# A fixed order of VectorE's work at the ends of sub-layers, and ten early products of constants, in a two-layer trunk

## The chip, the cores and the metric

The kernel runs on one core of one Trainium2 chip. Its time is the device time of one launch, in microseconds. Three runs of the kernel before took 2077.28, 2075.53 and 2076.88 us; the median is 2076.88 us. One more execution was recorded by the hardware profiler; it took 2074.67 us, and the trace spans 2072.9 us of that. Engines are called PE (matrix products; PEld is its weight load), DVE (VectorE), ACT (ScalarE), POOL (GpSimd) and SP (which here only issues transfers).

## The reference

A trunk of two layers works on x of 256 rows and 2048 columns in float32. Each layer has a mixer and a squared-ReLU MLP, and each of these four sub-layers ends in the same way:

```python
h = rms_norm(x, mix_pre_g[layer])
m = pool_conformer_mixer(...) if layer % 2 == 0 else short_conv_mixer(...)
x = x + rms_norm(m, mix_post_g[layer])
h = rms_norm(x, ffn_pre_g[layer])
x = x + rms_norm(sq_relu_mlp(h, ffn_w1[layer], ffn_w2[layer]), ffn_post_g[layer])
```

The first mixer projects h into three parts: one goes through causal means over 2, 4, 8 and 16 frames and a small product, the other two through a gate, a causal depthwise convolution of width 31, LayerNorm and swish; both results go through one output projection. The second mixer is `W_out(B * conv3(C * u))`. The MLP is 2048 to 8192 to 2048 with `relu(.)**2` between. `rms_norm` needs the sum of squares over a whole row of 2048, so no column of the next sub-layer can be started before the last column of this one is known.

## The kernel before, in words

The 256 rows are two tiles of 128 (`t` is 0 or 1, called row 0 and row 1 here). Every large product takes float32 operands as two parts, a high part `hi` and the remainder `lo`, and adds up three products: high by high, high by low and low by high (lines 224 to 226). Weights are streamed in segments of 128 x 1024 floats (512 KB): `prep_to` (L166) issues the transfer into `raw` on SP's queue (L170), ACT copies it to `whi` (L173), DVE subtracts to make `wlo` (L178; in part of the first mixer POOL does it). There are four `raw` buffers and nine of `whi` and `wlo` each. A block of 512 output columns of one row tile is one call of `mms`: three matmuls of 512 columns for each of its 8 or 16 pieces of 128 input rows, so 24 or 48 matmuls.

The order on each engine is not written by hand. The program is traced in Python order, and a scheduler then lays the instructions out by a model of their times: on each engine it takes the ready instruction of highest priority, which is the earliest traced one; `urgent` (L329) raises what it wraps by 150 places. The resulting queues are static and every engine works in order. `later` and `tick` (L197, L201) put small tasks, such as transposes, between the matmuls of following blocks.

At the end of a sub-layer, for each row tile, `mix_evac` or `last_evac` (L587, L654) handles each block of 512 columns: a sum of squares on ACT, and a product by the gain on DVE into `m` (L592 or L659). After the last block `mix_close` (L594) makes the row's factor: a square root on ACT and six small DVE operations (L600, L320 to L324). `close_row` (L343) then updates x in four pieces of 512 columns on DVE (L355), and for each piece `norm_chunk` (L293) has PE transpose it in four matmuls (L276), ACT write the high part `xh` (L262) and DVE the remainder `xl` (L265). The last blocks of a sub-layer are ordered so that row 0 is done 10.9 us of matmuls before row 1. The next sub-layer's first block is row 0's, by `mms_wide` (L229), which takes all products with the weights' high parts first (L240, L241), and those with the low parts last (L248). There are three such ends inside the run (layer 0's mixer, layer 0's MLP, layer 1's mixer), called ends A, B and C here, and the end of the program.

In layer 0's mixer, `pool_sum` (L448) forms the causal means by products with a constant matrix, multiplies by `inv_cnt` on DVE (L463) into an SBUF tile, splits that (`split_plain`, L270: ACT L271, DVE L272), and `pool_mix` (L478) multiplies the two parts (L492). `ln_stats` and `ln_apply` do the LayerNorm with products by a constant matrix `ones` of 1/1024 (L547, L560). The last projection of this mixer adds a block to its earlier part in `opart` (L647) and goes over the column blocks and row tiles in the order (2,0), (2,1), (3,0), (3,1), (0,0), (1,0), (0,1), (1,1).

Of the kernel before, what the change touches and what calls it, by code (L numbers as in the profile page):

```python
# [16 lines left out]
P = 128  # L17
# [16 lines left out]
def trunk_kernel(  # L34
# [19 lines left out]

    uid = [0]
# [103 lines left out]
    pool_lo = set()  # L159
    for key in ("f1_0_0_0", "sC0", "f1_1_0_0"):  # L160
        pool_lo |= set()
# [4 lines left out]
    def prep_to(i):  # L166
        while nxt[0] <= min(i, len(specs) - 1):
            src, nj = specs[nxt[0]]
            raw = wp.tile([P, 2 * CB], F32, tag="raw", name=nm("raw"), bufs=4)
            nc.sync.dma_start(raw.rearrange("p (j n) -> p j n", j=nj), src)  # L170
            hi = wp.tile([P, 2 * CB], F32R, tag="whi", name=nm("whi"))
            lo = wp.tile([P, 2 * CB], F32R, tag="wlo", name=nm("wlo"))
            act.copy(hi, raw)  # L173
            i_, on_pool = nxt[0], nxt[0] in pool_lo

            def low(raw=raw, hi=hi, lo=lo, on_pool=on_pool, eng=lo_eng[0](i_)):
                for s in ((slice(0, CB), slice(CB, 2 * CB)) if on_pool else (slice(None),)):
                    (pool if on_pool else eng).tensor_tensor(  # L178
                        lo[:, s], raw[:, s], hi.bitcast(F32)[:, s], ALU.subtract)

            low()
            wt[i_] = (hi, lo)
            nxt[0] += 1

    AHEAD = 8
    URGENT = 150
# [70 lines left out]
    def split_cols(p, col0, dst, scale_cols):  # L257

        hi, lo = dst
        for j in range(4):  # L260
            pj = p[:, j * P : (j + 1) * P]
            act.activation(hi[:, col0 + j, :], pj, AF.Copy, scale=scale_cols[j])  # L262
        for j in range(4):
            pj = p[:, j * P : (j + 1) * P]
            dve.scalar_tensor_tensor(  # L265
                lo[:, col0 + j, :], pj, scale_cols[j], hi[:, col0 + j, :].bitcast(F32),
                ALU.mult, ALU.subtract,
            )

# [23 lines left out]
    def norm_chunk(t, c, gkey, gbase):  # L293
        p = pst()
        transpose4(xs[t][:, c * CB : (c + 1) * CB], p)
        split_cols(p, 4 * (c % 2), xT[t, c // 2], [pcol(gkey, gbase + 4 * c + j) for j in range(4)])
# [46 lines left out]
    def close_row(t, s, nxt_gain, final=False):  # L343
# [3 lines left out]
        for c in range(4):  # L347
            cs = slice(c * CB, (c + 1) * CB)
            if final and c == 0:
                for q in (slice(0, CB // 2), slice(CB // 2, CB)):  # L350
                    dve.scalar_tensor_tensor(xs[t][:, q], ms[t][:, q], s, xs[t][:, q],
                                             ALU.mult, ALU.add)
                    nc.sync.dma_start(out[t * P : (t + 1) * P, q], xs[t][:, q])
                continue
            dve.scalar_tensor_tensor(xs[t][:, cs], ms[t][:, cs], s, xs[t][:, cs], ALU.mult, ALU.add)  # L355
# [23 lines left out]

    first()  # L380
# [59 lines left out]
    def load_pool():  # L440
        for s in range(2):
            raw = wp.tile([P, 2 * CB], F32, tag="raw", name=nm("rw"), bufs=4)
# [3 lines left out]
            pwin.append(w)  # L446

    def pool_sum(g):  # L448

        ic = t512((P, T))  # L450
        nc.sync.dma_start(ic, inv_cnt[g * T : (g + 1) * T].partition_broadcast(P))
        p = pst()
        for c in range(2):
# [8 lines left out]
        pd = t512((P, 2, T))  # L462
        dve.tensor_tensor(  # L463
            pd, p.rearrange("p (c n) -> p c n", c=2),
            ic.unsqueeze(1).to_broadcast([P, 2, T]), ALU.mult,
        )
        ph = tp.tile([P, 2, T], F32R, tag="ph", name=nm("ph"), bufs=2)
        pl = tp.tile([P, 2, T], F32R, tag="pl", name=nm("pl"), bufs=2)
# [125 lines left out]
    def mix_close(t, parts, nxt_gain, final=False):  # L594
# [7 lines left out]
        close_row(t, r, nxt_gain, final)  # L602
# [32 lines left out]
    for cb, t in ((2, 0), (2, 1), (3, 0), (3, 1), (0, 0), (1, 0), (0, 1), (1, 1)):  # L635
# [7 lines left out]
        else:  # L643
# [3 lines left out]
            dve.tensor_tensor(o, ps, o, ALU.add)  # L647
            ps = o
        urgent(mix_evac, t, cb, ps, gps[cb], parts)
        if cb == 1:  # L650
            urgent(mix_close, t, parts, ("ffn_pre", 0))
# [9 lines left out]
    def ffn(l, nxt_gain, final=False):  # L661
# [5 lines left out]
        for e in range(NE):  # L667
# [33 lines left out]
            for cb, t in order:  # L701
# [14 lines left out]
                if cb == NCB - 1:  # L716
                    urgent(mix_close, t, parts, nxt_gain, final)
# [63 lines left out]
    for cb in range(NCB):  # L781
        ids = seg[f"so{cb}"]
        gp = post_gain(mix_post_g, 1, cb)
        for t in range(NT):
# [4 lines left out]
            if cb == NCB - 1:  # L789
                urgent(mix_close, t, parts, ("ffn_pre", KT))  # L790
# [44 lines left out]
```

## Time and profile before

| what | value |
|---|---|
| median of 3 runs | 2076.88 us (2075.53 to 2077.28) |
| profiled execution: time, span of the trace | 2074.67 us, 2072.9 us |
| mean granted PE clock | 0.995 |
| PE busy, PEld busy | 2041.4 us (98%), 1687.7 us (81%) |
| DVE, ACT, POOL busy | 1174.0 us (57%), 1008.3 us (49%), 153.5 us (7%) |
| transfers | 390.30 MB at 188 GB/s mean |
| matmuls recorded | 9253 |

The trace's times are microseconds from its first instruction. A duration of a matmul in the trace is longer than the distance to the next one, since matmuls are pipelined; the price of a matmul is therefore read from the distance between starts. In the rows of waits, the engine and line that waited stand left of the arrow and what it waited for stands right of it.

### The profile page before, as it was taken

What the parts mean: (1) busy time and instruction counts of PE and PEld (TensorE: products, weight loads), DVE (VectorE), ACT (ScalarE), POOL (GpSimd) and SP (SyncE); (2) the same over time, 40 slices, a digit from 0 to 9 for tenths busy, and PEclk for the clock granted to TensorE, in tenths of its full rate; (3) what the DMA queues carried; (4) which work ended last, traced back from release to release, by engine and by line L of the source; (5) the groups of instructions that cost most, each with busy time, mean ns of one, the idle gap of its engine ahead of it and who ended that gap; (6) DMA issues with size and microseconds to landing.
All of it is one profiled execution on the core that took longest, in us unless ns stands there. A gap on an engine that the chain in (4) does not pass through costs nothing.

```text
span 2072.9 us, 24556 instructions
## 1 busy us (share of the span) xinstructions
PE 2041.4 (98%) x9253; PEld 1687.7 (81%) x9253; DVE 1174.0 (57%) x1522; ACT 1008.3 (49%) x1296; POOL 153.5 (7%) x83
## 2 busy tenths in 40 slices
PE   8999999999999999999999999999999999999998
PEld 7888778888888888887888888888888888888886
DVE  3797764455455455547655645674555464554545
ACT  6454664444444354445544444464544444353443
POOL 5887000000000000000000000000000000000000
PEclk9999999999999999999999999999999999999999
DMA  7665546556565556556454665655555565565653
GB/s 261 198 208 180 176 148 219 175 180 210 171 203 181 184 194 198 186 170 213 161 197 165 201 197 177 202 189 193 183 193 193 170 212 187 171 208 189 201 172 114
DMA packets 203078, 390.30 MB, mean 188 GB/s; under 512 B 12368, under 2 KB 14512, under 8 KB 202960
## 3 DMA queue, kind: packets, MB, share of 16 engines
q1 hardware_dynamic: 202656, 388.55, 56.7%
q8 instruction: 72, 1.18, 0.2%
q14 instruction: 46, 0.38, 0.1%
q0 software_dynamic: 256, 0.18, 0.0%
q10 hardware_dynamic: 48, 0.02, 0.0%
HBM read 386.60 MB, written 2.10 MB: 188 GB/s over the span
## 4 chain that ended last, share of the span: by engine, by line
PE 85%; DVE 2%; DMA 1%; issue 1%; ACT 0%; DVEq 0%; ACTq 0%
PE pg L224 27%; PE pg L226 27%; PE pg L225 27%; PE pt L276 2%; DVE wlo L178 1%; DVE x L355 1%; PE pg L248 1%; PE pg L241 0%; DMA gp<-in_mix_post_g_dram 0%; PE pg L240 0%; DMA raw<-in_ab_w_out_dram 0%; ACT whi L173 0%; DVE xl L265 0%; DMA raw<-in_sc_w_in_dram 0%; DVE m L592 0%
## 5 line engine op out<-in xcount | busy, mean ns | idle before, releaser
L178 DVE TENSOR_TENSOR wlo<-raw,whi 128x1024 fp32r<-128x1024 f32 x660 | 807.5, 1227 | 580.4 <-ACT whi L173 547.9
L173 ACT CAST whi<-raw 128x1024 fp32r<-128x1024 f32 x722 | 760.2, 1054 | 575.2 <-PE pg L226 383.1
L226 PE MATMUL pg<-whi,xl 128*128 128x512 f32 x1520 | 596.0, 393 | 0.0
L224 PE MATMUL pg<-whi,xh 128*128 128x512 f32 x1520 | 590.9, 390 | 0.8 <-ACT t L518 0.7
L225 PE MATMUL pg<-wlo,xh 128*128 128x512 f32 x1520 | 591.3, 390 | 0.0
L225 PE MATMUL pg<-wlo,ah 128*128 128x512 f32 x1024 | 398.3, 389 | 0.0
L224 PE MATMUL pg<-whi,ah 128*128 128x512 f32 x1024 | 398.1, 389 | 0.0
L226 PE MATMUL pg<-whi,al 128*128 128x512 f32 x1024 | 397.6, 391 | 0.0
L225 PEld LDWEIGHTS pg<-wlo,xh 128*128 128x128 f32 x1520 | 285.4, 188 | 59.1
L224 PEld LDWEIGHTS pg<-whi,xh 128*128 128x128 f32 x1520 | 285.5, 188 | 58.5 <-ACT t L518 1.1
L226 PEld LDWEIGHTS pg<-whi,xl 128*128 128x128 f32 x1520 | 285.4, 188 | 56.9
L225 PEld LDWEIGHTS pg<-wlo,ah 128*128 128x128 f32 x1024 | 192.2, 188 | 40.1
L224 PEld LDWEIGHTS pg<-whi,ah 128*128 128x128 f32 x1024 | 192.3, 188 | 39.3
L226 PEld LDWEIGHTS pg<-whi,al 128*128 128x128 f32 x1024 | 192.3, 188 | 39.3
L178 POOL TENSOR_TENSOR wlo<-raw,whi 128x1024 fp32r<-128x1024 f32 x62 | 147.7, 2421 | 46.4 <-ACT whi L173 46.1
L680 ACT ACTIVATE t<-pg,rr 128x512 f32<-128x512 f32 x64 | 43.9, 686 | 194.0 <-PE pg L226 192.8
L711 DVE TENSOR_TENSOR m<-pg,m 128x512 f32<-128x512 f32 x96 | 65.9, 687 | 74.6 <-PE pg L226 74.6
L224 PE MATMUL pg<-whi,yh 128*128 128x512 f32 x256 | 100.2, 392 | 1.6 <-ACT yh L271 1.5
L225 PE MATMUL pg<-wlo,yh 128*128 128x512 f32 x256 | 99.7, 390 | 0.0
L226 PE MATMUL pg<-whi,yl 128*128 128x512 f32 x256 | 98.5, 390 | 0.2 <-DVE yl L272 0.2
L421 DVE SCALAR_TENSOR_TENSOR acc<-pp,par,acc 128x256 f32<-128x256 f32 x240 | 96.3, 480 | 0.1
L272 DVE TENSOR_TENSOR al<-pt,ah 128x512 fp32r<-128x512 f32 x64 | 44.0, 688 | 74.8 <-ACT ah L271 74.7
(130 smaller groups left out, 902.9 us busy)
## 6 DMA issues: line engine op xcount, KB each, us to landing
raw<-in_ffn_w_dram SPq DMA_DIRECT2D x512, 512.0 KB, 4.7
raw<-in_sc_w_in_dram SPq DMA_DIRECT2D x96, 512.0 KB, 4.9
raw<-in_ab_w_in_dram SPq DMA_DIRECT2D x48, 512.0 KB, 4.6
raw<-in_ab_w_out_dram SPq DMA_DIRECT2D x32, 512.0 KB, 3.9
raw<-in_sc_w_out_dram SPq DMA_DIRECT2D x32, 512.0 KB, 5.4
x<-in_x_dram SPq DMA_DIRECT2D x8, 256.0 KB, 7.2
gp<-in_mix_post_g_dram SPq DMA_DIRECT2D x8, 256.0 KB, 5.9
gp<-in_ffn_post_g_dram SPq DMA_DIRECT2D x8, 256.0 KB, 4.6
```

What stands on the lines that cost most here:

```text
L173: act.copy(hi, raw)
L178: (pool if on_pool else eng).tensor_tensor(lo[:, s], raw[:, s], hi.bitcast(F32)[:, s], ALU.subtract)
L224: pe.matmul(ps, lh, wh, start=start and k == 0, stop=False)
L225: pe.matmul(ps, lh, wl, start=False, stop=False)
L226: pe.matmul(ps, ll, wh, start=False, stop=stop and k == n - 1)
L248: pe.matmul(ps, lhs(k)[0], wt[c][1][:, j * CB : (j + 1) * CB], start=False, stop=k == n - 1)
L272: dve.tensor_tensor(lo, src, hi.bitcast(F32), ALU.subtract)
L276: pe.transpose(p[:, j * P : (j + 1) * P], src[:, j * P : (j + 1) * P], ident)
L355: dve.scalar_tensor_tensor(xs[t][:, cs], ms[t][:, cs], s, xs[t][:, cs], ALU.mult, ALU.add)
L421: dve.scalar_tensor_tensor(a, src, wcol, a, ALU.mult, ALU.add)
L680: act.activation(rl, ps, AF.Relu, scale=rr[t])
L711: dve.tensor_tensor(dst, ps, dst, ALU.add)
```

## The change

- At the three inner ends, DVE gets a fixed order by scheduling edges that cost no semaphore. Of the nine weight segments that come first in the next sub-layer, `wlo` of numbers 1 to 4 come after row 0's second x update, and those of numbers 5 to 8 after the last remainder `xl` of row 0; row 1's first x update also comes after that last remainder. Number 0 is left free.
- `urgent` raises by 1000 places and not by 150, and now also wraps L647, which writes its sum into the PSUM bank and not into `opart`.
- There are six `raw` buffers. The first two segments of the next sub-layer at ends A and B take their `hi` and `lo` from the three buffers of tags `ah` and `al`, which hold activations elsewhere.
- `inv_cnt` is loaded in `load_pool`, two transfers in place of four, into the two buffers that the post gains use; `pool_sum` multiplies inside the PSUM bank, and its parts `ph` and `pl` lie among the `t512` tiles.
- The last projection of layer 0's mixer goes (2,0), (3,0), (2,1), (3,1), and then as before.
- Before the first transfers have landed, PE gets ten products of `ones` by `ones` into a bank that nothing reads.
- After the row factors of the start, a one-column sigmoid on ACT.

```diff
-            raw = wp.tile([P, 2 * CB], F32, tag="raw", name=nm("raw"), bufs=4)
+            raw = wp.tile([P, 2 * CB], F32, tag="raw", name=nm("raw"), bufs=RAW)      # RAW = 6
...
-            hi = wp.tile([P, 2 * CB], F32R, tag="whi", name=nm("whi"))
-            lo = wp.tile([P, 2 * CB], F32R, tag="wlo", name=nm("wlo"))
+            home, tags = (ap_, ("ah", "al")) if nxt[0] in guests else (wp, ("whi", "wlo"))
+            hi = home.tile([P, 2 * CB], F32R, tag=tags[0], name=nm("whi"))
+            lo = home.tile([P, 2 * CB], F32R, tag=tags[1], name=nm("wlo"))
...
+    guests = set(seg["f1_0_0_0"][:2]) | set(seg["sC0"][:2])
+    def after(inst, first):
+        tc.add_manual_dep(
+            inst.ins, first.ins.name,
+            mybir.DependencyInfo(mybir.DependencyClass.NoSync, mybir.DependencyReason.SCHED_ONLY),
+            reason="row chain first")
+    def hold(ids, first):
+        for i in ids:
+            if i in lows:
+                after(lows[i], first)
+            else:
+                guards[i] = first
...
-    URGENT = 150
+    URGENT = 1000
...
-            dve.scalar_tensor_tensor(xs[t][:, cs], ms[t][:, cs], s, xs[t][:, cs], ALU.mult, ALU.add)
+            upd = dve.scalar_tensor_tensor(xs[t][:, cs], ms[t][:, cs], s, xs[t][:, cs],
+                                           ALU.mult, ALU.add)
+            if nxt_ids:
+                if t == 0 and c == 1:
+                    hold(nxt_ids[1:5], upd)
+                if t == NT - 1 and c == 0:
+                    after(upd, split_end[0])
...
+                    end = urgent(norm_chunk, t, c, *nxt_gain)
+                    if t == 0 and c == 3:
+                        split_end[0] = end
+                        hold(nxt_ids[5:], end)
...
+    idle = pst()
+    for i in range(10):
+        pe.matmul(idle[:, :P], ones, ones, start=i == 0, stop=i == 9)
     first()
...
     for t in range(NT):
         row_scale(t)
+    act.activation(small(), rr[NT - 1], AF.Sigmoid)
...
+        for h in range(2):
+            ic = mp.tile([P, 2 * T], F32, tag="gp", name=nm("ic"))
+            nc.sync.dma_start(ic, inv_cnt[2 * h * T : 2 * (h + 1) * T].partition_broadcast(P))
...
-        pd = t512((P, 2, T))
-        dve.tensor_tensor(
-            pd, p.rearrange("p (c n) -> p c n", c=2),
-            ic.unsqueeze(1).to_broadcast([P, 2, T]), ALU.mult,
-        )
-        ph = tp.tile([P, 2, T], F32R, tag="ph", name=nm("ph"), bufs=2)
-        pl = tp.tile([P, 2, T], F32R, tag="pl", name=nm("pl"), bufs=2)
+        pd = p.rearrange("p (c n) -> p c n", c=2)
+        dve.tensor_tensor(pd, pd, ic.unsqueeze(1).to_broadcast([P, 2, T]), ALU.mult)
+        ph, pl = t512((P, 2, T), F32R), t512((P, 2, T), F32R)
         split_plain(pd, ph, pl)
...
-    for cb, t in ((2, 0), (2, 1), (3, 0), (3, 1), (0, 0), (1, 0), (0, 1), (1, 1)):
+    for cb, t in ((2, 0), (3, 0), (2, 1), (3, 1), (0, 0), (1, 0), (0, 1), (1, 1)):
...
-            dve.tensor_tensor(o, ps, o, ALU.add)
-            ps = o
+            urgent(dve.tensor_tensor, ps, ps, o, ALU.add)
```

More of the change, by code (lines that the diff above doesn't have):

```diff
@@ L157, in trunk_kernel @@
     add_ffn(1)
[L159 to L161 removed]
+    lows, guards = {}, {}
+    guests = set(seg["f1_0_0_0"][:2]) | set(seg["sC0"][:2])
[10 more added lines that the diff above has]
+                guards[i] = first
     wt = {}
@@ L168, in prep_to @@
             src, nj = specs[nxt[0]]
-            raw = wp.tile([P, 2 * CB], F32, tag="raw", name=nm("raw"), bufs=4)
+            raw = wp.tile([P, 2 * CB], F32, tag="raw", name=nm("raw"), bufs=RAW)
             nc.sync.dma_start(raw.rearrange("p (j n) -> p j n", j=nj), src)
-            hi = wp.tile([P, 2 * CB], F32R, tag="whi", name=nm("whi"))
-            lo = wp.tile([P, 2 * CB], F32R, tag="wlo", name=nm("wlo"))
+            home, tags = (ap_, ("ah", "al")) if nxt[0] in guests else (wp, ("whi", "wlo"))
+            hi = home.tile([P, 2 * CB], F32R, tag=tags[0], name=nm("whi"))
+            lo = home.tile([P, 2 * CB], F32R, tag=tags[1], name=nm("wlo"))
             act.copy(hi, raw)
[L174 to L181, printed above, removed]
+            i_ = nxt[0]
+            low = lo_eng[0](i_).tensor_tensor(lo, raw, hi.bitcast(F32), ALU.subtract)
+            lows[i_] = low
+            if i_ in guards:
+                after(low, guards[i_])
             wt[i_] = (hi, lo)
@@ L264, in split_cols @@
             pj = p[:, j * P : (j + 1) * P]
-            dve.scalar_tensor_tensor(
+            low = dve.scalar_tensor_tensor(
                 lo[:, col0 + j, :], pj, scale_cols[j], hi[:, col0 + j, :].bitcast(F32),
@@ L268, in split_cols @@
             )
+        return low
     def split_plain(src, hi, lo):
@@ L295, in norm_chunk @@
         transpose4(xs[t][:, c * CB : (c + 1) * CB], p)
-        split_cols(p, 4 * (c % 2), xT[t, c // 2], [pcol(gkey, gbase + 4 * c + j) for j in range(4)])
+        return split_cols(p, 4 * (c % 2), xT[t, c // 2],
+                          [pcol(gkey, gbase + 4 * c + j) for j in range(4)])
     def sumsq(parts):
@@ L441, in load_pool @@
         for s in range(2):
-            raw = wp.tile([P, 2 * CB], F32, tag="raw", name=nm("rw"), bufs=4)
+            raw = wp.tile([P, 2 * CB], F32, tag="raw", name=nm("rw"), bufs=RAW)
             nc.sync.dma_start(raw, pool_win[:, s * 1024 : (s + 1) * 1024])
@@ L446, in load_pool @@
             pwin.append(w)
+        for h in range(2):
+            ic = mp.tile([P, 2 * T], F32, tag="gp", name=nm("ic"))
+            nc.sync.dma_start(ic, inv_cnt[2 * h * T : 2 * (h + 1) * T].partition_broadcast(P))
+            icnt[h] = ic
     def pool_sum(g):
-        ic = t512((P, T))
-        nc.sync.dma_start(ic, inv_cnt[g * T : (g + 1) * T].partition_broadcast(P))
+        ic = icnt[g // 2][:, (g % 2) * T : (g % 2 + 1) * T]
         p = pst()
```

22 lines of the change are left out of this document (14 added, 8 removed).

## The prediction

> **What bounds the kernel now.** I read the page's busy shares first, then the waits of PE, then PE's order of time around each wait, and last DVE's rows at the same places.
>
> ```profile
> PE 2041.4 (98%) x9253; PEld 1687.7 (81%) x9253; DVE 1174.0 (57%) x1522; ACT 1008.3 (49%) x1296; POOL 153.5 (7%) x83
> ```
>
> PE is busy for 98% of the span, so time can only be won where PE stands still or runs at a lower clock. The next view says for whom it stands.
>
> ```profile
> PE pg L241 <- DVE xl L265: 5.8, 4, 2.7
> PE pt L101 <- DMA t<-in_mix_pre_g_dram: 4.6, 1, 4.6
> PE pg L240 <- ACT xh L262: 4.0, 2, 2.2
> PE pt L492 <- DVE pl L272: 2.5, 1, 2.5
> PE pg L224 <- ACT yh L271: 1.5, 1, 1.5
> ...
> PE pg L224 <- ACT t L518: 0.7, 1, 0.7
> ```
>
> Apart from the first transfer (4.6 us, L101), the waits are those of row 0's `xh` and `xl` at the inner ends (9.8 us), the means (2.5), the LayerNorm (1.5) and a sigmoid (0.7). Waits alone understate an end, because the clock drops too. So I price PE's work there. These rows, sixteen matmuls in a run of which the first and the last are shown, and a group of transposes in plain running, give the prices.
>
> ```profile
> 975.76 0.39 PE L226 MATMUL pg<-whi,al 128*128 128x512 f32 x1
> ...
> 979.16 0.39 PE L226 MATMUL pg<-whi,al 128*128 128x512 f32 x1
> ```
>
> ```profile
> 297.37 0.39 PE L224 MATMUL pg<-whi,xh 128*128 128x512 f32 x1
> 297.60 0.60 PE L276 MATMUL pt<-ident,t 128*128 128x128 f32 x4
> 297.95 0.48 PE L225 MATMUL pg<-wlo,xh 128*128 128x512 f32 x1
> 298.27 0.39 PE L226 MATMUL pg<-whi,xl 128*128 128x512 f32 x1
> ```
>
> A matmul costs (979.16 - 975.76) / 15 = 0.2267 us. A group of four transposes costs (298.27 - 297.37) - 2 x 0.2267 = 0.45 us. The three stretches from the last matmul before ends A, B and C to the start of L248 (busy time, count, granted clock, share and rate of transfers):
>
> ```profile
> 256.77:274.60 17.83, 12.85 (x57) 0.81 0.56 175
> 979.39:997.12 17.73, 12.83 (x58) 0.81 0.53 169
> 1344.35:1356.69 12.34, 11.45 (x58) 1.00 0.95 313
> ```
>
> At A and B the stretch holds 32 matmuls of `mms_wide` and six groups of transposes: 32 x 0.2267 + 6 x 0.45 = 9.95 us. A loses 17.83 - 9.95 = 7.9 us and B 7.8 us. At C it holds 41 matmuls and four groups, 11.1 us, and loses 1.2 us. Together 16.9 us are lost. PE's own rows show where:
>
> ```profile
> 257.45 1.32 PE L276 MATMUL pt<-ident,x 128*128 128x128 f32 x8 [0.53 <-DVE x L355]
> 261.01 0.80 PE L240 MATMUL pg<-whi,xh 128*128 128x512 f32 x1 [2.24 <-ACT xh L262]
> 263.76 0.79 PE L241 MATMUL pg<-whi,xl 128*128 128x512 f32 x1 [1.96 <-DVE xl L265]
> ...
> 979.98 1.29 PE L276 MATMUL pt<-ident,x 128*128 128x128 f32 x8 [0.44 <-DVE x L355]
> 983.04 0.51 PE L240 MATMUL pg<-whi,xh 128*128 128x512 f32 x1 [1.76 <-ACT xh L262]
> 986.21 0.80 PE L241 MATMUL pg<-whi,xl 128*128 128x512 f32 x1 [2.66 <-DVE xl L265]
> ```
>
> The reason is how late DVE gets to row 0's x update. The first three rows below are where row 0's last block left PE, the next three its first x update at A, B, C.
>
> ```profile
> 246.08 0.69 DVE L647 TENSOR_TENSOR opart<-pg,opart 128x512 f32<-128x512 f32 x1 [2.23 <-PE pg L226]
> ...
> 968.71 0.70 DVE L656 TENSOR_TENSOR pg<-pg,m 128x512 f32<-128x512 f32 x1 [2.52 <-PE pg L226]
> ...
> 1335.77 0.60 ACT L591 ACTIVATE junk<-pg 128x512 bf16<-128x512 f32 x1 [6.68 <-PE pg L226]
> ```
>
> ```profile
> 256.65 2.73 DVE L355 SCALAR_TENSOR_TENSOR x<-m,sm,x 128x512 f32<-128x512 f32 x4
> ...
> 979.09 2.73 DVE L355 SCALAR_TENSOR_TENSOR x<-m,sm,x 128x512 f32<-128x512 f32 x4
> ...
> 1339.30 2.74 DVE L355 SCALAR_TENSOR_TENSOR x<-m,sm,x 128x512 f32<-128x512 f32 x4
> ```
>
> That is 10.6 us at A, 10.4 at B, but 3.5 at C. Between the two, at A, DVE did this:
>
> ```profile
> L178 DVE TENSOR_TENSOR wlo<-raw,whi 128x1024 fp32r<-128x1024 f32 x5 | 6.1, 1215 | 0.0
> L592 DVE TENSOR_TENSOR m<-opart,gp 128x512 f32<-128x512 f32 x2 | 1.4, 690 | 1.8 <-DMA gp<-in_mix_post_g_dram 1.8
> ```
>
> Five low halves of weights, 1.2 us each, had filled the gaps of a chain of small operations, and one gain came 1.8 us late. Of nine weight buffers eight hold the two running column blocks, so these five are next-layer numbers 1 to 5: those that the edges hold back.
>
> **The change, part by part.**
>
> *Holds, URGENT, six `raw` buffers, guests (ends A, B, C).* Without fillers row 0's first update comes as at C plus the extra addition of 0.7 us, 4.2 us after PE: 250.3 at A, 972.9 at B. All four updates end 2.7 us later, 253.0 and 975.6. What is late next is the splits, which now share DVE with numbers 1 to 4 (4.9 us together). From update to use a chunk takes 4.4 us (256.65 to 261.01 above), so the last is ready by 253.0 + 4.4 + 4.9 = 262.3 at A even if all four low halves stand ahead of it. PE, whose last matmul moves from 256.8 to 258.6 with four transpose groups (1.8 us) now ahead of it, needs that last chunk after 24 more matmuls, at 264.0. Row 1's chain starts at 258.6 and gives its first chunk 4.2 + 4.4 us later, at 267.2; PE gets there after 48 matmuls, at 269.5: room for one low half, nearly two. Numbers 5 to 8 come after row 0's last split and number 5 is first read at 258.6 + 42 x 0.2267, 268.1. SP's queue waits for `raw` buffers, which held low halves keep; the two extra buffers and the two guests pay for that. The gain late by 1.8 us goes too, if `m` of block (3,1) isn't queued behind a weight. The bounds are 0 and 16.9 us; the nearest row is C, where a chain started 3.5 us after PE cost 1.2 us. I leave 0.9 at A, 0.9 at B and 0.4 at C: 16.9 - 2.2 = 14.7 us won.
>
> *The means.* In the four `pl` rows the two SBUF operands make the time uneven; the product out of a bank at the same time is not slowed:
>
> ```profile
> L272 DVE TENSOR_TENSOR pl<-t,ph x4: 683/1161/2657, 137.4 to 165.8; 128x512 fp32r<-128x512 f32 x4
> ...
> 164.00 0.68 DVE L463 TENSOR_TENSOR t<-pt,t 128x512 f32<-128x512 f32 x1
> ```
>
> With `pd` in the bank I take 0.68 for the 2.66: 2.0 us of PE's 2.5 us wait (bounds 0 and 2.5). The gains' buffers, lent to `inv_cnt`, are last read near 164.00, 82 us before row 0's last block at 246.08, so this costs nothing; without that cover the gains would come late, as at A now by 1.8 us. `ph` and `pl` in `t512` hold two of six tiles for longer; I price that at nothing, since the tiles for `ic` and the product are given up for them.
>
> *The sigmoid.* It moves this load to the start:
>
> ```profile
> 56.06 1.28 ACT L518 ACT_TABLE_LOAD   x1
> ```
>
> The 0.7 us wait goes. Bounds: +0.7, and -0.6 if all 1.3 us of the load fall in PE's way at the start; taken +0.6, since ACT is busy for 49% of the time.
>
> *The order of blocks.* Both row 0 blocks get ahead of the LayerNorm of row 1. The scheduler could do that already; bounds 0 and 1.5 us (the `yh` wait), taken 0.4.
>
> *Ten products.* A product by `ones` is two recorded matmuls (16 products here are 32), and sixteen of those take 1.95 us at full clock.
>
> ```profile
> L547 PE MATMUL pt<-cs__424,ones x32: 270/275/275, 181.4 to 191.5; 128*128 128x128 f32 x32
> ...
> 189.84 1.95 PE L547 MATMUL pt<-cs__424,ones 128*128 128x128 f32 x16
> ```
>
> ```profile
> 0.87 0.20 POOL L83 MEMSET ones<- 128x128 f32 x1
> ...
> 4.56 0.28 PE L101 MATMUL pt<-ident,t 32*128 32x32 f32 x1 [4.56 <-DMA t<-in_mix_pre_g_dram]
> ...
> 6.91 1.09 PE L276 MATMUL pt<-ident,x 128*128 128x128 f32 x4 [1.02 <-DMA x<-in_x_dram]
> ```
>
> At the start four transposes take 1.09 us where 0.60 is usual, so PE runs at about half clock. Twenty matmuls cost 20 x 0.12 x 1.8 = 4.3 us from 1.1 us on, to 5.4: up to 0.9 us past the 4.56 at which PE starts now, if the clock stays low; if it rises, two groups of transposes are 0.5 us cheaper each. Bounds -0.9 and +1.0, taken +0.2. How the clock behaves is seen at end A:
>
> ```profile
> 256.40:259.78 3.38, 1.84 (x11) 0.94 (x9) 3.38 (x7) 1.55 (x3) 0.00 (x0) 1.00 0.88 247
> 259.78:263.20 3.42, 0.80 (x1) 0.29 (x1) 3.42 (x5) 3.42 (x11) 0.00 (x0) 0.50 0.85 263
> ```
>
> A stretch of 3.4 us with PE half idle is followed by one at 0.50. The Trainium skill, page "TensorE: Matmul & The Clock Gate", section "What's actually happening", says that the clock is released after one window of about 3.4 us of activity, in windows that run freely, and falls back after an idle one; A's rows agree. By that rule the products raise the clock before the first real matmul, the term is +1.0 and the sum below 0.8 us larger. The same page's section "Part 4: PE-mode transpose" speaks against it: transposes don't count as activity, so the clock may fall again before the first real matmul, which would make the term -0.9 and the sum 1.1 us smaller; no run here shows that yet.
>
> *Sum.* 14.7 + 2.0 + 0.6 + 0.4 + 0.2 = 17.9 us. The profiled execution took 2074.67 us, so 2056.8; the median of the runs is 2.2 us above it, so **2059.0 us**.
>
> **The rivals.**
>
> *The ends are only half mended (17 in 100).* Row 0's transposes, raised by 1000, stand in PE's static queue where the plan puts them; where the real x update comes later, PE waits in the middle of row 1's matmuls. For it: at A the plan was early by 0.5 us. Against it: C, where the updates came 3.5 us after PE, kept its clock at 1.00 and lost little. If A and B keep half (3.9 us each) and C all its 1.2, the ends give 7.9 us (16.9 - 9.0), the means 2.0: 2067 us.
>
> *The edges don't do it (5 in 100).* Other low halves fill the gaps, and only the side terms stay, 3.2 us: 2073.7 us, inside the 0.2% (4.2 us) that a measurement of this kernel can tell from no change. Against it: the five fillers are just the ones held.
>
> *ACT stands at a guest (8 in 100, slower).* A guest's `whi` needs a buffer of tag `ah`, and at A and B two of three are in use until row 0's or row 1's last block is done. If the plan puts that ACT copy ahead of row 0's sum of squares and the buffer comes free only with row 1's last matmul, row 0's chain starts at 256.8 and 979.4, with first updates 4.2 us later, at 261.0 and 983.6: 4.4 and 4.5 us later than now. With the 3.2 us of side terms: 2076.9 + 8.9 - 3.2 = 2082.6 us. It decides once the copy waits as long as row 1 is behind row 0, over 10 us at both ends; half of that only undoes the gain. Against it: row 0's last block frees a buffer at 246.08 + 0.69 = 246.8, as its chain begins.
>
> **How the numbers follow.** The forecast has 70 in 100, the rivals 17, 5 and 8. The forecast's own range is 2053 to 2063: all upper bounds together are 16.9 + 2.5 + 0.7 + 1.5 + 1.0 = 22.6 us, 2054.3, less 1.4 us, which the lowest run is below the median; downwards another 4 us for splits that come late at two ends. The range for 8 in 10 reaches to the first rival: 2052 to 2069, leaving out the other two and a little of the first. Faster by over 0.2%: 0.70 + 0.17 = 0.87; within: 0.05; slower: 0.08.
>
> **What would show it.** In the profile after, row 0's first L355 should start 3.5 to 5 us after its last block at A and B, with no L178 between but number 0's; the stretches to L248 should lose under 1.5 us each and show a granted clock of 1.00; the L492 wait should be under 0.6 us; the sigmoid's table load should be gone from 56 us. The prediction is wrong if PE waits for x (L276) among row 1's matmuls, if ACT stands at a `whi` copy while row 0's squares are due, or if PE waits for `wlo` in L248.

## The result, and the profile after

Four runs of the changed kernel took 2063.41 to 2066.18 us, median 2064.54; four of the kernel before have a median of 2076.89. The ratio is 0.9942, with a 95% interval of 0.9925 to 0.9960: the change wins 12.3 us. The forecast was 2059.0, the range 2052 to 2069, with 0.87 on faster. The time lies inside that range and 1.5 us outside the forecast's own one (2053 to 2063). The profiled execution took 2064.32 us, 10.35 less than the one of before (2074.67); the sections below divide up this smaller difference.

The page's busy times, and the waits of PE:

```profile
PE 2041.5 (99%) x9273; PEld 1689.2 (82%) x9273; DVE 1170.8 (57%) x1522; ACT 1006.9 (49%) x1297; POOL 152.6 (7%) x83
```

```profile
PE pg L255 <- DVE xl L279: 3.9, 4, 1.4
PE pg L238 <- ACT yh L286: 2.1, 1, 2.1
PE pg L254 <- ACT xh L276: 1.8, 2, 1.2
...
PE pg L238 <- ACT t L551: 0.6, 1, 0.6
```

PE does the same work with fewer gaps. The waits at the ends (`xl`, `xh`) fell from 9.8 to 5.7 us; the one for the means is gone; the one for `yh` in the LayerNorm has *grown* from 1.5 to 2.1; the sigmoid's still costs 0.6. (Line numbers moved: L238 to L240 are the old L224 to L226, L254, L255 and L262 the wide block's old L240, L241 and L248, L291 the transposes, L276 `xh`, L279 `xl`, L192 the low halves, L373 the x update, L350 the addition that was L647, L625 and L689 the old L592 and L656.)

Both kernels run the same 8640 matmuls of 512 columns, so the start of the n-th in one trace can be set against the n-th in the other. This gives the shift by section, in us against before (negative is won); the sections end at matmuls 180, 600, 680, 930, 1400 (end A lies in this one), 4500 (end B) and 6000 (end C). Each row is one profiled execution, worked out from the trace:

| kernel | time, us | start | sigmoid | means | LayerNorm | A | B | C | all |
|---|---|---|---|---|---|---|---|---|---|
| changed | 2064.54 | -1.3 | -0.1 | -2.3 | +0.5 | -2.7 | -3.4 | -1.2 | -10.5 |
| e1 no edges | 2074.35 | -1.6 | -0.4 | -2.3 | +0.6 | +2.9 | -0.4 | +0.6 | -0.5 |
| e2 copies held | 2064.41 | -1.5 | -0.3 | -2.3 | +2.1 | -2.2 | -6.1 | -0.2 | -10.4 |
| e3 early transposes | 2062.32 | -1.5 | -0.1 | -2.3 | +0.6 | -4.0 | -4.4 | -0.7 | -12.5 |
| e4 no products, no sigmoid, old order | 2059.92 | +0.5 | -1.0 | -2.3 | -2.8 | -4.0 | -4.0 | -1.2 | -14.9 |
| e5 old order | 2062.62 | -1.4 | -0.4 | -2.3 | 0.0 | -3.1 | -3.9 | -1.2 | -12.2 |
| e6 e5 + e3 | 2061.97 | -1.4 | -0.3 | -2.3 | 0.0 | -3.5 | -4.6 | -0.8 | -12.9 |
| e7 e6, low halves later | 2070.35 | 0.0 | -0.9 | -2.3 | 0.0 | -1.6 | -0.1 | +0.3 | -4.7 |
| e8 no sigmoid | 2067.83 | -1.2 | +1.3 | -2.3 | +2.2 | -2.8 | -3.5 | -1.2 | -7.6 |
| e9 no products | 2060.16 | +0.1 | -1.0 | -2.3 | -2.8 | -4.0 | -4.3 | -1.2 | -15.4 |
| e10 load behind `yh` | 2061.98 | -0.3 | -0.9 | -2.3 | -0.9 | -2.8 | -4.0 | -1.2 | -12.4 |
| e11 e6 + e10 | 2061.07 | -1.4 | -0.1 | -2.3 | -1.2 | -3.6 | -4.3 | -0.7 | -13.5 |
| e12 e11, no products | 2059.39 | +0.1 | -1.0 | -2.3 | -2.8 | -3.8 | -4.7 | -0.7 | -15.2 |

The time is the median of the runs; for e1 to e4 it is that of the profiled execution alone. The kernel before had a median of 2076.68 to 2077.24 beside them.

**The ends.** The first part of DVE's chain did what the prediction said. Row 0's last block and first x update on DVE's timeline, at A and at B:

```profile
242.90 0.70 DVE L350 TENSOR_TENSOR pg<-pg,opart 128x512 f32<-128x512 f32 x1 [2.98 <-PE pg L240]
245.43 0.69 DVE L625 TENSOR_TENSOR m<-pg,gp 128x512 f32<-128x512 f32 x1 [1.83 <-DMA gp<-in_mix_post_g_dram]
...
247.44 2.74 DVE L373 SCALAR_TENSOR_TENSOR x<-m,sm,x 128x512 f32<-128x512 f32 x4
250.10 3.49 DVE L192 TENSOR_TENSOR wlo<-raw,whi 128x1024 fp32r<-128x1024 f32 x3
253.50 0.69 DVE L350 TENSOR_TENSOR pg<-pg,opart 128x512 f32<-128x512 f32 x1
254.10 1.21 DVE L192 TENSOR_TENSOR wlo<-raw,whi 128x1024 fp32r<-128x1024 f32 x1
255.24 0.69 DVE L350 TENSOR_TENSOR pg<-pg,opart 128x512 f32<-128x512 f32 x1
255.84 2.14 DVE L279 SCALAR_TENSOR_TENSOR xl<-pt,par,xh 128x128 fp32r<-128x128 f32 x8
...
962.83 0.70 DVE L689 TENSOR_TENSOR pg<-pg,m 128x512 f32<-128x512 f32 x1 [2.98 <-PE pg L240]
966.41 2.74 DVE L373 SCALAR_TENSOR_TENSOR x<-m,sm,x 128x512 f32<-128x512 f32 x4
```

The update stands 4.5 us (A) and 3.6 us (B) behind the block, with no low half between, where it was 10.6 and 10.4. But the gain did not arrive at PE. From the first product of the wide block (L254) to the first with a low part (L262) there are 32 matmuls and two groups of transposes, 32 x 0.2267 + 2 x 0.45 = 8.15 us. The three stretches (length, busy times, granted clock, transfers):

```profile
254.48:267.74 13.26, 9.41 (x41) 6.56 (x40) 10.46 (x31) 10.98 (x30) 0.00 (x0) 1.00 0.45 157
974.41:986.85 12.44, 10.59 (x41) 7.76 (x40) 9.61 (x30) 10.06 (x26) 0.00 (x0) 0.86 0.43 147
1338.05:1346.60 8.55, 8.52 (x42) 6.71 (x40) 6.96 (x20) 6.86 (x21) 0.00 (x0) 1.00 0.41 136
```

C loses 0.4 us, A still 5.1 and B 4.3. PE's timeline at A shows for whom:

```profile
252.91 1.04 PE L291 MATMUL pt<-ident,x 128*128 128x128 f32 x8
...
256.23 0.50 PE L255 MATMUL pg<-whi,xl 128*128 128x512 f32 x1 [1.36 <-DVE xl L279]
...
257.73 0.60 PE L291 MATMUL pt<-ident,x 128*128 128x128 f32 x4
...
260.03 0.60 PE L291 MATMUL pt<-ident,x 128*128 128x128 f32 x4
...
261.51 0.50 PE L254 MATMUL pg<-whi,xh 128*128 128x512 f32 x1 [0.64 <-ACT xh L276]
262.67 0.50 PE L255 MATMUL pg<-whi,xl 128*128 128x512 f32 x1 [0.66 <-DVE xl L279]
...
265.97 0.50 PE L255 MATMUL pg<-whi,xl 128*128 128x512 f32 x1 [1.19 <-DVE xl L279]
```

x was ready from 248.2 on, yet its transposes wait in PE's queue until 252.91, behind row 1's matmuls. DVE has four low halves ahead of the first `xl` (255.84). Three of them are done by 253.6, when ACT begins the first `xh` (253.55), so only the fourth and two additions (L350) stand in its way.

Only two of row 0's four chunks are transposed ahead of the wide block. The other two stand inside it, at 257.73 and 260.03. There are two banks for transposes (the pool `ps_t`), so chunk 2 needs the bank that the first four `xl` read; but PE's rows show no wait there, so what sets the time is the place in the queue. Then ACT does weight copies ahead of chunk 2's `xh`; ACT's timeline:

```profile
258.60 1.12 ACT L190 CAST whi<-raw 128x1024 fp32r<-128x1024 f32 x1
260.14 1.05 ACT L190 CAST whi<-raw 128x1024 fp32r<-128x1024 f32 x1 [0.42 <-DMA raw<-in_ffn_w_dram]
261.09 1.14 ACT L276 ACTIVATE xh<-pt,par 128x128 fp32r<-128x128 f32 x4
...
262.29 1.16 ACT L276 ACTIVATE xh<-pt,par 128x128 fp32r<-128x128 f32 x4
```

And DVE does two of row 1's x updates (L373) ahead of the last chunk's `xl`:

```profile
262.26 1.12 DVE L279 SCALAR_TENSOR_TENSOR xl<-pt,par,xh 128x128 fp32r<-128x128 f32 x4 [2.46 <-ACT xh L276]
...
264.24 1.42 DVE L373 SCALAR_TENSOR_TENSOR x<-m,sm,x 128x512 f32<-128x512 f32 x2
265.57 0.86 DVE L279 SCALAR_TENSOR_TENSOR xl<-pt,par,xh 128x128 fp32r<-128x128 f32 x3
266.35 0.74 DVE L373 SCALAR_TENSOR_TENSOR x<-m,sm,x 128x512 f32<-128x512 f32 x1
267.01 0.34 DVE L279 SCALAR_TENSOR_TENSOR xl<-pt,par,xh 128x128 fp32r<-128x128 f32 x1
267.27 0.74 DVE L373 SCALAR_TENSOR_TENSOR x<-m,sm,x 128x512 f32<-128x512 f32 x1
```

The edge on row 1's first x update was meant to keep row 1 behind row 0's last remainder. It holds one update of four (`c == 0`, the first 512 columns), and the scheduler lets the other three go first, here and at B and C (from 983.87 and 1342.51). PE's wait of 1.19 us at 265.97 is for this `xl`.

At B the same gaps leave PE busy for 1.56 of 3.41 us, and the next 3.41 us run at half clock:

```profile
978.45:981.86 3.41, 1.56 (x8) 0.93 (x7) 1.49 (x5) 3.38 (x8) 0.00 (x0) 1.00 0.25 89
981.86:985.27 3.41, 3.41 (x9) 2.63 (x9) 3.18 (x11) 3.41 (x13) 0.00 (x0) 0.50 0.25 75
```

**The LayerNorm.** ACT's queue has the table load for the square root, and the square of block (3,0), ahead of both `yh` of row 1:

```profile
219.55 1.28 ACT L615 ACT_TABLE_LOAD   x1
...
220.95 0.58 ACT L624 ACTIVATE junk<-pg 128x512 bf16<-128x512 f32 x1
...
221.52 1.13 ACT L286 CAST yh<-t 128x512 fp32r<-128x512 f32 x2
```

**The start.** The ten products, as twenty matmuls, end at 5.77, and transposes behind them run at full clock (0.65 us for four, where it was 1.09):

```profile
1.14 4.63 PE L412 MATMUL pt<-ones 128*128 128x128 f32 x20 [1.14 <-POOL eps_t L86]
...
5.88 0.65 PE L291 MATMUL pt<-ident,x 128*128 128x128 f32 x4
```

### The profile page after: what moved, and what is told of

It is laid out like the page before. It is cut to its first block, busy times and chain, and to the rows that moved or that the text cites. A ratio compares the mean times of both kernels' runs of the same rounds, so it can differ in the third digit from the quotient of the medians.

```text
span 2062.5 us, 24574 instructions
## 1 busy us (share of the span) xinstructions
PE 2041.5 (99%) x9273; PEld 1689.2 (82%) x9273; DVE 1170.8 (57%) x1522; ACT 1006.9 (49%) x1297; POOL 152.6 (7%) x83
## 4 chain that ended last, share of the span: by engine, by line
PE 87%; DVE 1%; DMA 1%; ACT 0%; issue 0%; DVEq 0%; ACTq 0%
PE pg L240 28%; PE pg L238 28%; PE pg L239 28%; PE pt L291 2%; PE pg L262 1%; PE pg L255 0%; PE pg L254 0%; DMA raw<-in_sc_w_in_dram 0%; DVE x L373 0%; DMA raw<-in_ffn_w_dram 0%; DVE wlo L192 0%; ACT xh L276 0%; DVE xl L279 0%; ACT whi L190 0%; DVE pg L350 0%
## 5 line engine op out<-in xcount | busy, mean ns | idle before, releaser
L192 DVE TENSOR_TENSOR wlo<-raw,whi 128x1024 fp32r<-128x1024 f32 x660 | 805.0, 1226 | 501.2 <-ACT whi L190 460.5
L190 ACT CAST whi<-raw 128x1024 fp32r<-128x1024 f32 x722 | 759.3, 1055 | 465.7 <-PE pg L240 426.5
L240 PE MATMUL pg<-whi,xl 128*128 128x512 f32 x1520 | 595.9, 393 | 0.0
L238 PE MATMUL pg<-whi,xh 128*128 128x512 f32 x1520 | 590.7, 390 | 0.6 <-ACT t L551 0.6
L238 PE MATMUL pg<-whi,ah 128*128 128x512 f32 x1024 | 398.2, 389 | 0.0
L240 PE MATMUL pg<-whi,al 128*128 128x512 f32 x1024 | 397.2, 390 | 0.0
L238 PEld LDWEIGHTS pg<-whi,xh 128*128 128x128 f32 x1520 | 285.6, 188 | 57.9 <-ACT t L551 1.0
L240 PEld LDWEIGHTS pg<-whi,xl 128*128 128x128 f32 x1520 | 285.4, 188 | 57.1
L238 PEld LDWEIGHTS pg<-whi,ah 128*128 128x128 f32 x1024 | 192.3, 188 | 39.4
L240 PEld LDWEIGHTS pg<-whi,al 128*128 128x128 f32 x1024 | 192.3, 188 | 39.4
L192 POOL TENSOR_TENSOR wlo<-raw,whi 128x1024 fp32r<-128x1024 f32 x62 | 146.7, 2411 | 43.6 <-ACT whi L190 43.5
L286 ACT CAST ah<-pt 128x512 fp32r<-128x512 f32 x64 | 37.5, 585 | 135.2 <-PE pt L291 134.8
L238 PE MATMUL pg<-whi,yh 128*128 128x512 f32 x256 | 100.3, 393 | 2.2 <-ACT yh L286 2.1
L240 PE MATMUL pg<-whi,yl 128*128 128x512 f32 x256 | 98.3, 390 | 0.2 <-DVE yl L287 0.2
```

Of the source, the lines that this page charges most:

```text
L192: low = lo_eng[0](i_).tensor_tensor(lo, raw, hi.bitcast(F32), ALU.subtract)
L238: pe.matmul(ps, lh, wh, start=start and k == 0, stop=False)
L240: pe.matmul(ps, ll, wh, start=False, stop=stop and k == n - 1)
L286: act.copy(hi, src)
```

## Experiments

**e1: are the edges what won the ends?** Theory E says yes; its rival U says that URGENT, the buffers and the guests did it.

```diff
-            if nxt_ids:
-                if t == 0 and c == 1:
-                    hold(nxt_ids[1:5], upd)
-                if t == NT - 1 and c == 0:
-                    after(upd, split_end[0])
...
-                        hold(nxt_ids[5:], end)
```

> The changed kernel without the scheduling edges on DVE: neither low halves nor row 1's update are held back; URGENT 1000, six raw buffers, guests and all the rest stay. Theory E (the edges won the 6.1 us of ends A and B and the 1.2 us of C): the low halves fill the gaps of row 0's chain again, the first x update of row 0 comes about 10 us after its last block at A and B, and the gains of the ends over the kernel before fall from 2.7, 3.4 and 1.2 us to under 1 us each. Rival U (the higher urgency, the raw buffers and the guests won them): the three gains stay within 1 us of the changed kernel's.

Measured: 2074.35 us. The ends are 10.4 us worse than with the edges (5.6, 3.0 and 1.8), and A is worse than before. Without the edges the other parts win nothing at the ends, so the gain needs the edges; whether the edges would win it without the other parts, no run shows. Its waits of PE also show where the forecast's first rival lives:

```profile
PE pt L291 <- DVE x L373: 4.6, 1, 4.6
```

PE stood 4.6 us at a transpose for x that was late: the plan had put it early, and the low halves had moved x to 257.10. With the edges this wait does not occur.

**e2: ACT's copies of numbers 5 to 8 held behind row 0's last `xh`.**

```diff
-            act.copy(hi, raw)
+            cast = act.copy(hi, raw)
+            copies[i_] = cast
+            if i_ in cguards:
+                after(cast, cguards[i_])
...
+                        for i in nxt_ids[5:]:
+                            if i in copies:
+                                after(copies[i], last_hi[0])
+                            else:
+                                cguards[i] = last_hi[0]
```

> One more edge in the changed kernel: ACT's copies (whi) of next-layer segments 5 and later come after row 0's last xh. Theory A (what is left at A and B is ACT's order: the copies stand in front of xh of chunks 2 and 3): PE's waits for xh and xl in the second half of the wide block shrink from 2.5 us at A and 1.9 us at B to under 0.8 us, the half clock at B goes, and A and B win 2 and 3 us more. Rival D (what is left is DVE's order: four low halves stand in front of row 0's first xl): no more than 0.5 us at either.

Measured: 2064.41 us, no gain in sum. B wins 2.7 us more and loses its half clock, A and C lose 0.5 and 1.1 (at A with a half-clock stretch, 266.1 to 269.5, that the changed kernel does not have), and the LayerNorm, which the edit does not touch, 1.6 (half clock from 221.7 to 225.1). PE now waits for the copies themselves, 3.8 us in three places (`whi`, L190 of the changed kernel). ACT's order does matter at B, but holding all four copies only moves the wait.

**e3: row 0's first transposes earlier in PE's queue.** Row 1's last block goes on from its fifth piece only behind row 0's transposes of chunks 0 and 1.

```diff
-                pe.matmul(ps, lh, wh, start=start and k == 0, stop=False)
+                mm = pe.matmul(ps, lh, wh, start=start and k == 0, stop=False)
+                if gate and gate[0][0] <= k:
+                    after(mm, gate.pop(0)[1])
...
+                    if nxt_ids and t == 0 and c < 2:
+                        gate.append(((4, 4)[c], last_tr[0]))
```

> Edges on PE in the changed kernel: the last block of row 1 goes on after a third of its matmuls only when row 0's transposes of chunks 0 and 1 have been issued, which puts them 10 to 14 matmuls earlier in PE's queue. Theory P (PE's static queue holds the transposes 4 us longer than x needs): the chunks follow one another earlier and A and B win 2 us each, C about nothing. Rivals A and D: under 0.7 us at each end, because ACT's copies or DVE's low halves still stand in between; if x is later than the queue, PE waits and the ends get slower.

Measured: 2062.32 us; A and B win 1.3 and 1.1 us more, C loses 0.5. That lies between theory P (2 us each) and its rivals (under 0.7). PE's place for the transposes is a cause, but not the largest: the first `xl` at A comes at 255.12 in place of 255.84, still behind four low halves.

**e4: products, early sigmoid and block order undone.**

```diff
-    idle = pst()
-    for i in range(10):
-        pe.matmul(idle[:, :P], ones, ones, start=i == 0, stop=i == 9)
...
-    act.activation(small(), rr[NT - 1], AF.Sigmoid)
...
-    for cb, t in ((2, 0), (3, 0), (2, 1), (3, 1), (0, 0), (1, 0), (0, 1), (1, 1)):
+    for cb, t in ((2, 0), (2, 1), (3, 0), (3, 1), (0, 0), (1, 0), (0, 1), (1, 1)):
```

> Three small parts undone together, each read at its own place: no products of ones, no early sigmoid, and the old order of the blocks of layer 0's mixer. Products: if they raise the clock early, the first matmuls fall back by 1.3 us (half clock until about 10 us); if the earlier start has another reason, such as the order of ACT, by under 0.4 us. Sigmoid: the gain of 0.1 us near matmul 192 goes, nothing more. Old order: if the new order cost the 0.5 us between the means and end A, that comes back; if the LayerNorm's own chain did, it stays within 0.2 us.

Measured: 2059.92 us, *faster* than the changed kernel. The start loses 1.8 us. The section of the sigmoid wins 0.9, where a loss of 0.1 was expected, and the LayerNorm and end A, which products and sigmoid are far from, win 3.3 and 1.3. I put this down to the old block order; e5 tests that.

**e5: the old block order alone** (the last two lines of e4's diff).

> The changed kernel with the blocks of the mixer's last product in the order of before, (2,0), (2,1), (3,0), (3,1); products, early sigmoid and everything at the ends stay. Theory O: the new order itself costs the LayerNorm, because ACT's queue then has the square of block (3,0) and a table load ahead of yh. Then the section from the means to the LayerNorm's product wins the 3.3 us by which it was shorter in e4 (-2.8 against before, in place of +0.5), yh L286 stands near 219.0 ahead of the table load, and the median is 2064.5 - 3.3 = 2061.2 us, at end A 2060 to 2062. Rival: e4 won there because its plan was another without the products and the early sigmoid. Then the section stays near +0.5, and the median near 2064.5, over 2063.5 us.

Measured: 2062.62 us (2062.55 to 2064.81), ratio 0.9933 (0.9920 to 0.9945). The LayerNorm wins 0.5 us, not 3.3, and ACT's load still stands ahead of `yh`. Theory O falls as the main cause: the new order costs the LayerNorm about half a microsecond there, and something else the rest. The rival's time, over 2063.5, did not come either. The runs overlap with those of the changed kernel (2063.41 to 2066.18), so the 1.9 us between the medians are not sharp.

**e6: e5 with e3's edges.**

> e5 with the edges of e3 (row 1's last block goes on behind row 0's transposes of chunks 0 and 1). If the two are independent, e3's gains come on top: A 1.3, B 1.1, C -0.5, in sum 1.9 us under e5, so near 2059.3 us by theory O. If both won the same time at end A (in e4 the old order alone had already brought A to -4.0, as much as e3 did), only B's 1.1 less C's 0.5 is left: 0.6 us under e5, near 2060.6.

Measured: 2061.97 us (2061.21 to 2062.70), 0.65 under e5: nearer to the second case, in which both won the same time at A. The two kernels' runs just overlap, so no more is read from it.

**e7: e6 with the low halves out of the way of the first `xl`.**

```diff
-                if t == 0 and c == 1:
-                    hold(nxt_ids[1:5], upd)
...
+                    if t == 0 and c == 1:
+                        hold(nxt_ids[1:5], end)
```

> e6 with the low halves of numbers 1 to 4 held behind row 0's last xl of chunk 1 in place of the second x update, and numbers 5 to 8 behind that of chunk 3. Theory D: in the changed kernel the three or four low halves (3.5 at A, 4.6 us at B) that DVE runs between row 0's updates and the first xl are what keeps row 0's splits late. Then the first xl comes 2 to 4 us earlier at A and B, PE's wait for xl at L255 falls from 4 us to under 1.5, and the median is 1.5 to 3 us under e6. Rival W: DVE had that time free, since the first xl waits for PE's transposes and ACT's xh; the low halves only move between xl of chunk 1 and xl of chunk 2, where they are in the way. Then the time stays within 0.7 us of e6 or is up to 2 us above it, with waits for xl of chunk 2 in place of chunk 0.

Measured: 2070.35 us (2069.14 to 2071.13), 8.4 slower than e6; both D and W miss. (About 0.8 us of it lie before the means, where this run's clock fell again; the last section shows that.) Half of D holds: the first `xl` at A comes at 252.60, and the wait for `xl` falls from 4.6 us to 1.8. But another wait, of 7.7 us, takes its place:

```profile
PE pt L296 <- DVE x L378: 7.7, 3, 3.5
PE pg L257 <- DVE xl L281: 1.8, 2, 0.9
```

DVE's timeline at A shows the low halves, now bunched, in the middle of row 1's chain, between two small operations of its factor:

```profile
262.44 0.15 DVE L343 RECIPROCAL sm<-sm 128x1 f32<-128x1 f32 x1
...
262.76 5.76 DVE L192 TENSOR_TENSOR wlo<-raw,whi 128x1024 fp32r<-128x1024 f32 x5
268.44 0.27 DVE L345 TENSOR_SCALAR sm<-sm,sm 128x1 f32<-128x1 f32 x1
...
270.25 2.74 DVE L378 SCALAR_TENSOR_TENSOR x<-m,sm,x 128x512 f32<-128x512 f32 x4
```

PE stands 3.36 us at row 1's transposes (271.06). So DVE cannot simply do the low halves later: what row 0 gains, row 1 loses. An edge that puts numbers 5 to 8 behind row 1's x updates as well was not tried.

**e8: the changed kernel without the early sigmoid.**

> The changed kernel without the sigmoid of the means' row at the start (its table is then loaded at the first real sigmoid, as before); the products and the new block order stay. If the early sigmoid is what costs the section after the start 0.9 us (-0.07 in the changed kernel, -0.98 in e4), that section wins 0.9 and the median is 2063.6 us, with a table load of 1.3 us back near 56 us. If that section of the changed kernel only gives back what the products win at the start (weights that come no earlier), the section stays at -0.1 and the median within 0.4 us of 2064.5. By my forecast's own term it would lose 0.6 us: 2065.1.

Measured: 2067.83 us (2067.18 to 2068.60), 3.3 slower than the changed kernel; none of the three expected times (2063.6, 2064.5, 2065.1) came. The section of the sigmoid loses 1.3 us (its table load is back at 56.13, and PE waits 2.0 us for `t` in place of 0.6). The LayerNorm loses 1.7 more: there PE's wait for `yh` is as long as in the changed kernel (2.1), but it falls so that the clock is at half from 224.1 to 227.5.

**e9: the changed kernel without the ten products** (the first lines of e4's diff).

> The changed kernel without the ten products; early sigmoid and new block order stay. Theory P: the ten products cost the LayerNorm. The plan counts them, everything behind them is planned later, and the changed plan puts ACT's table load (1.28 us) ahead of both yh. Without them the load stands between the first yh and the second. Then the start loses 1.8 us (+0.5 against before), the section to the LayerNorm wins 2.5 to 3.3 (-2.0 to -2.8), the wait for yh is under 0.5 us, and the median is 1 to 3 us under the changed kernel's 2064.5. Rival S: the early sigmoid or the new order is what costs there. Then the wait stays near 2.1, the section near +0.5, and the median rises by the lost start to 2065 to 2066.5.

Measured: 2060.16 us (2059.43 to 2060.97), ratio 0.9919 (0.9906 to 0.9933): 4.4 us faster than the changed kernel, whose four runs all lie above. The start loses 1.5 us, and what comes behind wins 6.3: 0.9 in the sigmoid's section, 3.3 in the LayerNorm, 1.3 at A, 0.9 at B. Theory P's mechanism holds; its size, 1 to 3 us, was too small. The wait for `yh` is gone from PE's list, and ACT's queue has the load behind the first `yh`:

```profile
218.65 0.62 ACT L286 CAST yh<-t 128x512 fp32r<-128x512 f32 x1 [0.24 <-DVE t L613]
219.29 1.28 ACT L612 ACT_TABLE_LOAD   x1
```

The traces show a second piece. The low half on DVE that stands ahead of row 0's variance, in the changed kernel and in e9:

```profile
194.39 3.28 DVE L192 TENSOR_TENSOR wlo<-raw,whi 128x1024 fp32r<-128x1024 f32 x1 [4.54 <-ACT whi L190]
...
194.17 1.97 DVE L192 TENSOR_TENSOR wlo<-raw,whi 128x1024 fp32r<-128x1024 f32 x1 [4.91 <-ACT whi L190]
```

In the changed kernel it starts 0.15 us after a low half on POOL, in e9 0.8 us before one. It takes 3.27 to 3.29 us in the kernel before and in all ten kernels with products, and 1.97 to 1.99 in the three changed ones without.

Not all of the 6.3 us is a price of the plan. The 0.9 in the sigmoid's section is the start's own gain given back: e7 and e10 have the products too, but their starts won 0.0 and 0.3, and their sections show the same -0.9, without the wait for `t` that the changed kernel has there. The 0.9 at B goes mostly with its half-clock stretch, which e5 and e10 are without as well (-3.9 and -4.0).

With the sigmoid and the new order in place, e9 equals e4 in every section within 0.4 us. So without the products these two edits together are worth nothing that shows; with them each had a price.

**e10: the products kept, and one edge that puts the load behind the first `yh`.**

```diff
-                act.activation(warm, sg[:, 0, 0:1], AF.Sqrt)
+                after(act.activation(warm, sg[:, 0, 0:1], AF.Sqrt), yh0)
```

> The changed kernel with one more edge: the square root that calls for the table load comes behind row 1's first yh on ACT. Nothing else changes. By theory P the place of the load in ACT's queue is all that the products cost here: the wait for yh falls from 2.1 to under 0.8 us, the section to the LayerNorm wins 1.3 to 3.3 us, and the median is near 2062.5, between 2061 and 2063.3. Rival Q: the LayerNorm's product is late for another reason (DVE's chain ends later by the plan), so the first yh comes only a little earlier: a gain under 0.7 us, 2063.8 or more.

Measured: 2061.98 us (2061.56 to 2062.39), ratio 0.9928 (0.9915 to 0.9940), 2.6 under the changed kernel. PE's wait for `yh` falls from 2.1 to 0.6 us and the LayerNorm wins 1.4 (from +0.5 to -0.9): the place of the load is a cause, shown by itself, of a little under half of that section's 3.3 us. Most of the rest is read from the trace only: the low half ahead of row 0's variance still takes 3.28 us here, 1.3 more than in e9. What costs A its 1.3 us was not taken apart. This run's start shows something else, on PE's timeline:

```profile
1.13 3.89 PE L413 MATMUL pt<-ones 128*128 128x128 f32 x20 [1.13 <-POOL eps_t L86]
...
5.12 0.66 PE L292 MATMUL pt<-ident,x 128*128 128x128 f32 x4
7.47 1.12 PE L292 MATMUL pt<-ident,x 128*128 128x128 f32 x4 [1.69 <-ACT par L103]
```

The products raised the clock, but it fell again before the first real matmul, and the start won 0.3 us in place of 1.3.

**e11 and e12: all that helped together, with and without the products.** e11 is e6 with e10's edge; e12 leaves the products out of e11.

> e6 (old block order, row 1's last block behind row 0's transposes) with the edge of e10. By theory P it wins e6's yh wait of 1.5 us: 2062.0 - 1.5 = 2060.5. By rival Q it stays over 2061.3. If the products also cost the section before and end A by the plan, e12 is still ahead of it by 1 us or more.

> e11 without the ten products: e4 with the early sigmoid, and with row 1's last block behind row 0's transposes. If the gains add up, e4's 2059.9 less the sigmoid's 0.3 to 1.3 and less e3's gain at B and C (0.6): 2058 to 2059. By rival S the early sigmoid brings the yh wait back, and it ends at 2061 or more. It is the version that I expect to beat both kernels by most.

Measured: 2061.07 us (2060.82 to 2061.32), ratio 0.9923 (0.9909 to 0.9936), and 2059.39 us (2058.78 to 2059.68), ratio 0.9914 (0.9901 to 0.9928). e11 lies between its theory (2060.5) and rival Q (over 2061.3); e12 is 0.4 over its expected range, and rival S's 2061 did not come. Without the products it is again 1.7 us faster. e12 is the fastest kernel here, 17.9 us under the one before beside it (2077.24) and, by medians, 5.2 under the changed one; e9, a single deletion from the changed kernel, comes within 0.8 us of it.

## Why the prediction was right, and where its sum was wrong

| term | forecast | section of the trace |
|---|---|---|
| ends A, B, C | 7.0, 6.9, 0.8: 14.7 | 2.7, 3.4, 1.2: 7.3 |
| means | 2.0 | 2.3 |
| sigmoid | 0.6 | 0.1 |
| order of blocks | 0.4 | -0.5 (LayerNorm) |
| products | 0.2 | 1.3 at the start |
| sum | 17.9 | 10.5 |

**Right.** The side was right for the reason given: low halves stood in the gaps of row 0's chain, and without the edges that take them out the ends are 10.4 us worse (e1), 3.1 of that worse than before. The update came 4.5 and 3.6 us after the block, where 3.5 to 5 was named. One sign failed: the stretches up to the low parts of the weights were to lose under 1.5 us each at a clock of 1.00, and they lose 5.1 at A and 4.3 at B, there at 0.86. The table load is gone from 56 us. The means' remainders (`pl`, now `t`) take the same time each, and PE's wait for them went:

```profile
L287 DVE TENSOR_TENSOR t<-pt,t x4: 681/682/684, 133.2 to 161.3; 128x512 fp32r<-128x512 f32 x4
```

Of the rivals, "ACT stands at a guest" and "the edges don't do it" did not happen. "Half mended" is near in its time (2067) but not in its mechanism: PE waited for x at a transpose in e1 and e7, not in the changed kernel.

**The step that failed** is the one on what is late next: "From update to use a chunk takes 4.4 us, so the last is ready by 262.3 at A even if all four low halves stand ahead of it." The first chunk kept to that: 8.8 us from update to the use of `xl` (247.44 to 256.23), where 4.4 + 4.9 = 9.3 were allowed. (The 4.4 were read at the use of `xh`, L240; to the use of `xl` the rows of before show 7.1, from 256.65 to 263.76.) The last chunk did not. All updates were done by 250.2, so by the same rule it was ready at 259.5; it was used at 265.97.

The sum put all four groups of transposes ahead of the wide block and let only DVE's low halves stand in the way. In the trace two groups go ahead. The last one stands in PE's queue until 260.03; its `xh` comes on ACT at 262.29, behind weight copies and the chunk before it; its `xl` on DVE at 265.57, behind row 1's factor and two of row 1's updates. e3 moves the first two groups forward and wins 1.3 and 1.1 us; e2 shows that ACT's copies count at B; e7 shows that DVE's low halves can be taken out of row 0, but land on row 1. How the 5.1 us of A divide among the three queues stays open; no run moved the last two groups or held all four of row 1's updates. The late gain, too, which I let go, still cost DVE 1.83 us at A. Part of the miss belongs to the products: in e9 the ends win 4.0, 4.3 and 1.2, in sum 9.4 and not 7.3.

**The products** were priced where they run. There they won 1.3 us, a little above the upper bound of 1.0. What the step left out is that the scheduler counts them too: the sections behind them cost 6.3 us against 1.5 won (e9). Of these 3.3 in the LayerNorm and 1.3 at A come with the changed orders, and 0.9 is the start's gain given back. This is the second mis-sized term: -4.4 by the medians, in place of +0.2.

**The sigmoid and the order of blocks** have no price of their own. The sigmoid is worth 3.3 us with the products (e8 against the changed kernel; 1.7 of it through a half-clock stretch elsewhere) and nothing that shows without them (e4 against e9, which differ in the order too). The new order costs 1.9 us by medians with the products (e5) and, by the same pair, nothing without.

The sum missed by 7.4 us, as much as the ends alone; the other terms cancelled. The median fell by 2.0 us more than the profiled execution did, so the forecast of the time missed by 5.5. That the time still lies in the range of 2052 to 2069 is partly luck: its upper part was there for the rival "half mended", whose mechanism the changed kernel does not show.

## What to carry to other kernels

Where a scheduler plans the queues, an edit costs what it does to the plan, also 200 us later on another engine: compare the time section by section, not only where the edit stands, and undo each small edit alone. When you make one operation of a chain earlier, follow the last piece of it, and not only the first, through every queue that it passes to the consumer: here the first chunk kept its allowance, and the last did not. An edge on the first of four like operations does not hold the other three. A filler that is moved out of one row's chain can land in the next one (e7); holding it behind both was not tried.

## What the runs showed of the hardware

What the ten products gained at the start went with the moment at which the full clock came, and that differed from one profiled execution to the next. Ten of the profiled kernels had the products. In eight the full clock came between 5.1 and 6.9 us and stayed; the start won 1.2 to 1.6 us. In two (e7 and e10) it came at 4.4 and 4.1, and the stretch after it (in e10 with PE busy for 1.72 of 3.41 us) was followed by one at half clock; they won 0.0 and 0.3 us. The three stretches in e10:

```profile
0.66:4.07 3.41, 2.94 (x14) 2.94 (x14) 0.00 (x0) 1.28 (x1) 3.02 (x9) 1.00 0.50 89
4.07:7.48 3.41, 1.72 (x14) 1.32 (x13) 0.12 (x1) 1.89 (x5) 2.21 (x5) 1.00 1.04 381
7.48:10.90 3.42, 3.42 (x10) 2.83 (x11) 3.33 (x10) 3.39 (x10) 0.00 (x0) 0.50 1.06 340
```

(The 1.00 of the first is no reading: the trace's first record of the clock is at 4.07, and the fourteen products before it took 0.21 us each, against 0.12 at full clock.) The kernels without products reached full clock at 10.6 to 12.0 us. Every half-clock stretch inside a run is 3.41 us long or a multiple of it. The Trainium skill, page "TensorE: Matmul & The Clock Gate", section "What's actually happening", says that the windows run freely, so the point of the change varies from run to run; the trace agrees, with full clock at 4.1 to 6.9 us for the same twenty matmuls. That spread of 2.8 us is wider than the 0.5 us to either side that the page gives.
